# A hybrid diffusion block on one core: the first FFN's last two blocks go down in one PSUM group, a third raw-weight buffer in the late heads, and the last norm divides before its transposes

## The chip, the cores and the metric

The kernel runs on one core of a Trainium2 chip. The metric is the device time of one execution, in microseconds (us), and the time shown is the median over several runs. A profile of one further execution gives the start and the length of each instruction on each engine. PE is TensorE (its weight loads are PEld), DVE is VectorE, ACT is ScalarE, POOL is GpSimd, and SP is SyncE, which here only issues transfers.

## The reference, cut to what matters

Two layers are computed over 512 latent tokens (x) and 256 context tokens (c) of width 1024. In the second layer the context is only read, and it gets no output.

```python
for l in range(DEPTH):                       # DEPTH = 2
    hx = _modulate(_rmsnorm(x, norm1_g[l]), sh1, sc1)
    hc = _modulate(_rmsnorm(cx, norm1_g[l]), csh1, csc1)
    ... = _split_heads(hx @ w_in[l], ...)     # w_in: 1024 x 2560
    x = x + g1 * _merge(na_x, diff_x, fux, ..., w_out[l])
    x = x + g2 * _conv_ffn(_modulate(_rmsnorm(x, norm2_g[l]), sh2, sc2), w_up[l], ..., w_down[l])
    if l < DEPTH - 1:                         # the same for the context tokens
        ...
def _conv_ffn(h, w_up, conv_w, conv_b, w_down):
    u = h @ w_up                              # w_up: 1024 x 5632
    u = up[:, :-2] * conv_w[0] + up[:, 1:-1] * conv_w[1] + up[:, 2:] * conv_w[2] + conv_b
    gate, val = jnp.split(u, 2, axis=-1)
    return (jax.nn.silu(gate) * val) @ w_down # w_down: 2816 x 1024
```

The six modulation vectors of a layer (sh1, sc1, g1, sh2, sc2, g2) come from `silu(c) @ w_mod[l] + b_mod[l]`, with w_mod 1024 x 6144.

## The kernel before, in words

Every large product is made of three matmuls: each operand is split into a rounded high part and the remainder as a low part (`split`: a cast on ACT, a subtraction on DVE or POOL), and high by high, high by low and low by high are summed in PSUM (`PASS`). Raw weights arrive by 1 MB transfers on SP's queue into tiles named `w`, which come from a pool `wp` of two buffers through a small class `Turn` that takes its pools in turn.

The instructions are not issued in program order. A planner orders each engine's instructions ahead of time by their place in the program and by times that it reckons; `tc.high_priority(tc.cur_priority - mark + ...)` moves a piece forward to the place noted in `mark`. On the chip each engine and each queue then takes its instructions strictly in the planned order.

**The modulation.** `w_mod` is multiplied in chunks of 512 columns (`mod_chunk`), two `w` tiles for each (`hf` 0 and 1) and eight small matmuls for each tile. `filler` does one chunk and finishes the chunk before it (`mod_finish`, line L184); it is called here and there to put this work between other work.

**The late heads.** The last four of the eight neighbourhood heads run while the modulation chunks for later use are multiplied (12 `w` tiles in layer 0, 8 in layer 1), followed by the four tiles of `w_out` (`out_weights`, L963). When they begin, the projection's buffers are closed and the freed memory goes to new pools (L1147 to L1159). Behind the heads, SP also loads six residual tiles in layer 0 (L1205), and then the output projection runs (L1233).

**The norms.** `norm_T` normalises token tiles and transposes them into 128-column pieces `k` = 0 to 7. The sum of squares is made on ACT (`stats`), and `spread` turns it into the reciprocal root `r`, spreads `r` along the tokens by a diagonal matrix and a matmul with ones (`bank`, L384) and copies it out (`rb`). For every `k`, `lift` transposes on PE, and `step` multiplies by `rb` and then by the modulation on DVE, casts the high part on ACT (L419) and makes the low part on POOL (L420), or on DVE for `k` = 3 and 7. In the second norm of layer 1 the tiles 0 to 2 go first (384 tokens) and tile 3 follows (128 tokens).

**The FFN.** It has 22 blocks `f` of 128 hidden columns, taken in pairs `j` = 0 to 10. `up_mm` makes `u` (x) and, in layer 0, `uc` (c); `conv` makes the gated product `gt` on ACT and DVE. `down` loads a pair's `w_down`, splits it into `wd`, and for each token tile (in layer 0 the two context tiles first, then the four x tiles) and each half of the columns sums six matmuls into one PSUM bank `dps`. The bank is multiplied by the gate into `dm` on DVE (L1362) and added to the residual `res` on POOL for the first half and on DVE for the second (L1363). Three banks are there for `dps` in layer 0, shared with the fillers. `down` of pair `j - 1` stands behind the up products of pair `j`; `down(9)` and `down(10)` are thus the last two, and behind them the first norm and projection of layer 1 begin (`bank`, L529: `hc` for context and `hx` for x).

Of the kernel before, what the change touches and what calls it, by code (L numbers as in the profile page):

```python
# [11 lines left out]
F32 = mybir.dt.float32  # L12
# [8 lines left out]
D = 1024  # L21
# [3 lines left out]
DEPTH = 2  # L25
# [24 lines left out]
def hybrid_kernel(ctx: ExitStack, tc: tile.TileContext, A, out, dbg=None, stop=None):  # L50
# [293 lines left out]
    def norm_T(l, which, xnp, hx, hc, pn, bank, wrap, cuts=((0, 4),), htile=None):  # L344
        hT = {0: [(hx[z] if isinstance(hx, list) else hx).tile([128, KT, 576 if wrap else 512], F32R, name=f"hx{z}")
                  for z in range(2)]}
        if hc:
            hT[1] = [hc.tile([128, KT, 256], F32R, name=f"hc{z}") for z in range(2)]
        tiles, ss, rb, tps = {}, {}, {}, {}

# [19 lines left out]
        def spread(v, i0, i1):  # L370
            n = i1 - i0
            x0 = xnp.tile([128, n], F32, tag=f"nx{n}", name="nx")
            ve.tensor_scalar(x0, ss[v][:, 0, i0:i1], 1.0 / D, EPS, op0=ALU.mult, op1=ALU.add)
            x = xnp.tile([128, n], F32, tag=f"ny{n}", name="ny")
            ve.scalar_tensor_tensor(x, ss[v][:, 1, i0:i1], 1.0 / D, x0, op0=ALU.mult, op1=ALU.add)
            r = rsqrt(x, "v" if which == 2 else None)
            if v not in rb:
                rb[v] = xnp.tile([128, 256 if v else 512], F32, tag=f"rb{v}", name="rb")
            dg = xnp.tile([128, 3, 128], F32, tag="dg", name="dg")[:, 0:n]
            ve.tensor_tensor(dg, idf.unsqueeze(1).to_broadcast([128, n, 128]),  # L380
                             r.unsqueeze(2).to_broadcast([128, n, 128]), op=ALU.mult)
            bc = bank(v)
            for i in range(n):
                pe.matmul(place(bc, v, i0 + i), lhsT=ones, rhs=dg[:, i], start=True, stop=True)  # L384
            cut_ = (lambda t: t[:, 0:256]) if v else CUT[i0, i1]
            sc.copy(cut_(rb[v]), cut_(bc))

        def lift(k, v, part=0):
            if (k, v, part) not in tps:
                tp = tps[k, v, part] = pn.tile([128, 256 if v else 512], F32, tag="n", name="ntp")  # L390
                for i in range(2) if v else range(*cuts[part]):
                    pe.transpose(place(tp, v, i), tiles[v][i][:, k * 128:(k + 1) * 128], idf)

        def step(k, v, part=0):
            lift(k, v, part)
            cut_ = (lambda t: t[:, 0:256]) if v else CUT[cuts[part]]
            tp, r = cut_(tps[k, v, part]), cut_(rb[v])
            n = 256 if v else 128 * (cuts[part][1] - cuts[part][0])
# [8 lines left out]
            w3 = [hT[0][z][:, k, 512:576] for z in range(2)] if wrap and v == 0 else []  # L407
            if k % 4 == 3:
                ve.scalar_tensor_tensor(h, tp, A_, r, op0=ALU.mult, op1=ALU.mult)
# [19 lines left out]
        def begin_x(xs):  # L429
            stats(0, xs)  # L430
            spread(0, 0, 3)
            lift(0, 0)
            spread(0, 3, 4)
# [24 lines left out]
    for l in range(DEPTH):  # L458
# [516 lines left out]
        with ExitStack() as es:  # L975
# [166 lines left out]
            for n, (h, i) in enumerate(steps):  # L1142
# [3 lines left out]
                if (he, ie) == (4, 0):  # L1146
# [9 lines left out]
                    open_rows(es, f"rp{l}", side="right")  # L1156
                    tqs.append(pool(es, f"tr{l}", 1, side="right"))
                    pt.pools += [pt.pools[0], pool(es, f"ptr{l}", 1, space=PSUM, side=SR)]
                    po.pools += [po.pools[0], pool(es, f"por{l}", 1, space=PSUM, side=SR)]  # L1159
# [31 lines left out]
            if first:  # L1191
                load_gate(g1, l, 2)

        es_att.close()
# [54 lines left out]
        with ExitStack() as es:  # L1249
# [91 lines left out]

            def down(j, gt):
                nonlocal mark
                w = wtile([128, 2, D])
                nc.sync.dma_start(w, A["w_down"][l, j * 256:(j + 1) * 256].rearrange("(k p) f -> p k f", p=128))
                wd = []
                for ff in range(2):
                    t = wdl.tile([128, 2, D], F32R, tag="wd", name="wd")
                    split(t[:, 0], t[:, 1], w[:, ff])
                    wd.append(t)  # L1350
                for t, key in order:
                    if t == 0:
                        mark = tc.cur_priority
                    for ch in range(2):
                        cs_ = slice(ch * 512, (ch + 1) * 512)
                        ps = pd.tile([128, 512], F32, tag="d", name="dps")
                        for ff in range(2):
                            for z, (a, b) in enumerate(PASS):
                                pe.matmul(ps, lhsT=gt[:, ff, a, t * 128:(t + 1) * 128], rhs=wd[ff][:, b, cs_],  # L1359
                                          start=ff == 0 and z == 0, stop=ff == 1 and z == 2)  # L1360
                        m = dmp.tile([128, 512], F32, tag="dm", name="dm")
                        ve.tensor_tensor(m, ps, g[:, 0 if key[0] == "x" else 1, cs_], op=ALU.mult)  # L1362
                        (gp if ch == 0 else ve).tensor_tensor(res[key][:, cs_], res[key][:, cs_], m, op=ALU.add)  # L1363
# [45 lines left out]
            for j in range(nj + 1):  # L1409
                if j < nj:  # L1410
# [3 lines left out]
                    for f in (2 * j, 2 * j + 1):  # L1414
# [8 lines left out]
                        elif f == 9:  # L1423
                            bias_scratch(l + 1, m)
                        elif f and f % 2 == 0:
                            filler((pd, "d"))
                            if f == 2:
                                filler((pd, "d"))
                if j > 0:
                    down(j - 1, gts[j - 1])  # L1430
        if dbg:
# [98 lines left out]
```

## Time and the profile before

| | |
|---|---|
| median of 3 runs | 1895.62 us (1895.04 to 1897.27) |
| the profiled execution's own time | 1893.96 us |
| its span, first to last instruction | 1892.2 us |
| PE busy | 1790.1 us (95% of the span) |
| DVE, ACT, POOL busy | 1284.0, 731.6 and 619.9 us |
| mean granted PE clock | 0.977 of full speed |

The profiled execution is 1.66 us (0.09%) below the median. Some 1.8 us of its time lie outside its span. Times of instructions are counted from the span's start: layer 0's attention ends at about 444, its output projection at 514, its FFN at 1117; layer 1's output projection runs from 1453 to 1498 and its FFN to the end.

### The profile page before, as it was taken

How to read it: one execution, taken by the hardware profiler on the slowest of the kernel's cores; microseconds unless marked ns; L12 is line 12 of the kernel's file. 1: busy time of each engine (PE TensorE's matmuls, PEld its weight loads, DVE VectorE, ACT ScalarE, POOL GpSimd, SP SyncE). 2: the span in 40 equal slices, each digit the busy share in tenths (PEclk: the TensorE clock that was granted, in tenths of full speed). 3: DMA queues.
4: the chain of work that ended last, by engine and by line, in shares of the span. 5: the costliest groups of instructions: out<-in, count | busy, mean ns of one | idle time of the engine just before them, and what ended most of it. 6: DMA issues, size and time to landing. Idle time of an engine off the chain costs nothing.

```text
span 1892.2 us, 27838 instructions
## 1 busy us (share of the span) xinstructions
PE 1790.1 (95%) x10817; PEld 1495.8 (79%) x10817; DVE 1284.0 (68%) x2561; ACT 731.6 (39%) x1335; POOL 619.9 (33%) x798
## 2 busy tenths in 40 slices
PE   6988999988999999999999989899999999999997
PEld 4787889856877888888888868788986778888885
DVE  4575865576465776677777695586658568777775
ACT  3325755454244222222232243475545243333331
POOL 2454646432141211211111154464733232122122
PEclk7998999999999999999999999999999999999999
DMA  9350021167015323423333012202234333232311
GB/s 282 118 177 24 31 55 32 34 211 209 28 45 187 126 95 103 161 73 106 112 112 112 23 51 95 89 24 61 55 110 137 100 112 112 89 112 90 94 41 45
DMA packets 146715, 183.04 MB, mean 97 GB/s; under 512 B 38200, under 2 KB 108672, under 8 KB 145560
## 3 DMA queue, kind: packets, MB, share of 16 engines
q1 hardware_dynamic: 107056, 157.83, 26.0%
q0 software_dynamic: 5888, 20.26, 3.5%
q10 hardware_dynamic: 33640, 3.19, 1.4%
q8 instruction: 85, 1.39, 0.3%
q14 instruction: 46, 0.38, 0.1%
HBM read 179.07 MB, written 8.07 MB: 99 GB/s over the span
## 4 chain that ended last, share of the span: by engine, by line
PE 79%; DVE 7%; DMA 6%; ACT 2%; issue 2%; POOL 2%; SPq 0%; ACTq 0%; DVEq 0%; POOLq 0%
PE u L1295 25%; PE dps L1359 14%; PE nacc L645 11%; PE uc L1295 7%; PE oacc L1233 5%; DMA w<-w_in 2%; PE bank L529 2%; PE m L143 2%; PE o L712 2%; PE s L1078 2%; DMA w<-w_out 2%; PE do L712 1%; PE tpp L1109 1%; PE dtpp L874 1%; PE ds L839 1%
## 5 line engine op out<-in xcount | busy, mean ns | idle before, releaser
L1295 PE MATMUL u<-hx,uwh 128*128 128x512 f32 (+2 forms) x2160 | 513.8, 391 | 7.1 <-ACT hx L419 2.7
L1295 PEld LDWEIGHTS u<-hx,uwh 128*128 128x128 f32 x2160 | 401.1, 189 | 98.0 <-ACT hx L419 3.6
L1363 POOL TENSOR_TENSOR res<-res,dm 128x512 f32<-128x512 f32 x110 | 157.3, 1431 | 586.1 <-DVE dm L1362 580.4
L1359 PE MATMUL dps<-wd,gt 128*128 128x512 f32 x1320 | 321.7, 393 | 6.8 <-DVE wd L75 3.0
L1359 PEld LDWEIGHTS dps<-wd,gt 128*128 128x128 f32 x1320 | 247.4, 189 | 62.8 <-DVE dm L1362 4.5
L645 PE MATMUL nacc<-wh,hx 128*128 128x256 f32 x1536 | 213.4, 291 | 3.8 <-ACT wh L71 3.1
L1324 DVE SCALAR_TENSOR_TENSOR ob<-u,cvc,ob 128x504 f32<-128x504 f32 x352 | 152.8, 476 | 89.7 <-ACT ob L1321 88.7
L645 PEld LDWEIGHTS nacc<-wh,hx 128*128 128x128 f32 x1536 | 196.7, 195 | 9.0 <-ACT wh L71 3.5
L1362 DVE TENSOR_TENSOR dm<-dps,g 128x512 f32<-128x512 f32 x220 | 147.7, 683 | 57.7 <-PE dps L1359 52.5
L1321 ACT ACTIVATE ob<-u,cvc 128x512 f32<-128x512 f32 x88 | 68.2, 777 | 195.8 <-PE u L1295 195.8
L1295 PEld LDWEIGHTS uc<-hc,uwh 128*128 128x128 f32 x1056 | 130.9, 190 | 7.4 <-issue 1.7
L1295 PE MATMUL uc<-hc,uwh 128*128 128x256 f32 x1056 | 134.3, 284 | 1.1 <-POOL hc L420 0.5
L75 POOL TENSOR_TENSOR wh<-w,wh 128x512 fp32r<-128x512 f32 x70 | 94.4, 1362 | 56.6 <-ACT wh L71 56.5
L71 ACT CAST uwh<-w 128x1024 fp32r<-128x1024 f32 x88 | 90.9, 1042 | 38.2 <-DMA w<-w_up 25.5
L1233 PE MATMUL oacc<-owh,yh 128*128 128x512 f32 x320 | 98.8, 397 | 5.9 <-ACT yh L71 3.2
L75 DVE TENSOR_TENSOR uwh<-w,uwh 128x1024 fp32r<-128x1024 f32 x74 | 97.0, 1317 | 8.8 <-ACT uwh L71 7.3
L1324 DVE SCALAR_TENSOR_TENSOR ob<-uc,cvc,ob 128x248 f32<-128x248 f32 (+1 forms) x176 | 53.0, 341 | 52.1 <-ACT ob L1320 51.5
L1363 DVE TENSOR_TENSOR res<-res,dm 128x512 f32<-128x512 f32 x110 | 87.2, 793 | 1.6
L645 PE MATMUL nacc<-wh,hc 128*128 128x256 f32 x624 | 88.1, 293 | 0.0
L71 ACT CAST gt<-g 128x768 fp32r<-128x768 f32 (+1 forms) x44 | 32.0, 727 | 136.5 <-DVE g L1339 136.5
L71 ACT CAST wd<-w 128x1024 fp32r<-128x1024 f32 x44 | 44.8, 1048 | 97.9 <-PE dps L1359 69.5
L645 PEld LDWEIGHTS nacc<-wh,hc 128*128 128x128 f32 x624 | 80.1, 196 | 2.7 <-issue 1.9
(527 smaller groups left out, 2872.7 us busy)
## 6 DMA issues: line engine op xcount, KB each, us to landing
w<-w_up SPq DMA_DIRECT2D x44, 1024.0 KB, 5.2
w<-w_mod SPq DMA_DIRECT2D x40, 1024.0 KB, 6.6
w<-w_down SPq DMA_DIRECT2D x22, 1024.0 KB, 5.0
w<-w_in SPq DMA_DIRECT2D x18, 1024.0 KB, 5.2
wm<-w_mod SPq DMA_DIRECT2D x8, 1024.0 KB, 9.9
w<-k_dftx POOLq DMA_DIRECT2D x8, 1024.0 KB, 5.2
w<-w_out SPq DMA_DIRECT2D x8, 1024.0 KB, 12.7
bS<-bT POOLq DMA_DIRECT2D x16, 360.0 KB, 9.1
```

What stands on the lines that cost most here:

```text
L71: r = sc.copy(dh, src)
L75: (gp if lo == "p" else ve).tensor_tensor(dl, src, dh.bitcast(F32), op=ALU.subtract)
L143: pe.matmul(m[32 * k:32 * k + 32, :], lhsT=cm[:, hf * 4 + k, :], rhs=w[:, k, :], start=hf == 0, stop=hf == 1)
L645: m = pe.matmul(acc[:, j], lhsT=col(hT[a], k, t + j), rhs=whs[k // 2][:, k % 2, b], start=k == 0 and z == 0, stop=k == KT - 1 and z == 2)
L712: m = pe.matmul(o[64 * half:64 * half + 64, 128 * b:128 * b + 128], lhsT=v, rhs=r, start=n == 0, stop=n == len(jobs) - 1)
L1233: pe.matmul(accs[t], lhsT=ys[k][a][:, t * 128:(t + 1) * 128], rhs=ow0[k // 2][:, k % 2, b], start=n == 0 and z == 0, stop=n == KT - 1 and ...
L1295: m = pe.matmul(u[2][:, 256 * v:256 * v + 256] if c else cut(u[v]), lhsT=whs[v][:, b, k], rhs=h2[c][a][:, k] if c else cut(h2[c][a][:, k]) ...
L1321: sc.activation(ob[:, 0:512], xu, AF.Identity, bias=b_, scale=w1)
L1324: ve.scalar_tensor_tensor(ob[:, d0:d0 + n], src[:, s0:s0 + n], w_, ob[:, d0:d0 + n], op0=ALU.mult, op1=ALU.add)
L1359: pe.matmul(ps, lhsT=gt[:, ff, a, t * 128:(t + 1) * 128], rhs=wd[ff][:, b, cs_], start=ff == 0 and z == 0, stop=ff == 1 and z == 2)
L1362: ve.tensor_tensor(m, ps, g[:, 0 if key[0] == "x" else 1, cs_], op=ALU.mult)
L1363: (gp if ch == 0 else ve).tensor_tensor(res[key][:, cs_], res[key][:, cs_], m, op=ALU.add)
```

## The change

Three edits are made at once.

The first is in layer 0's FFN. `down` is divided into `down_w` (load and split) and `down` (matmuls). The weights of pair 9 are prepared in their usual place, the weights of pair 10 go into the memory of the x tokens' low parts (`h2[0][1]`), and one `down` sums twelve matmuls to a bank for both pairs together. The fillers that stood behind blocks 18 and 20 move behind block 21, after `down_w(9)`.

The second is in both layers' late heads: a pool `wr` with one more raw buffer is appended to `wps`, so that tiles come in turn from `wp` and `wr`, and it is taken off again behind the heads.

The third is in the second norm of layer 1 (`early`). Each token tile is multiplied by its `r` on ACT, in two passes of 512 columns, into `xt`; the transposes read `xt`; `step` then has one DVE operation in front of the cast. The diagonal matrix, its matmuls and `rb` are not made there.

```diff
+        early = l == DEPTH - 1 and which == 2
...
             r = rsqrt(x, "v" if which == 2 else None)
+            if early:
+                for i in range(i0, i1):
+                    xt[v, i] = xnp.tile([128, D], F32, name=f"xt{v}{i}")
+                for c in range(0, D, 512):
+                    for i in range(i0, i1):
+                        sc.activation(xt[v, i][:, c:c + 512], tiles[v][i][:, c:c + 512], AF.Copy,
+                                      scale=r[:, i - i0:i - i0 + 1])
+                return
...
+            if early:
+                ve.tensor_scalar(h, tp, A_, B_, op0=ALU.mult, op1=ALU.add)
+                sc.copy(hi, h)
+                (ve if k % 4 == 3 else gp).tensor_tensor(lo, h, hi.bitcast(F32), op=ALU.subtract)
...
             spread(0, 0, 3)
-            lift(0, 0)
+            if not early:
+                lift(0, 0)
             spread(0, 3, 4)
...
+                    wps.pools.append(pool(es, f"wr{l}", 1, side="right"))
...
+            wps.pools[:] = [wp]
...
-            def down(j, gt):
+            def down_w(j, ts=None):
...
-                    t = wdl.tile([128, 2, D], F32R, tag="wd", name="wd")
+                    t = ts[:, ff] if ts else wdl.tile([128, 2, D], F32R, tag="wd", name="wd")
...
+            def down(wd):
...
-                        for ff in range(2):
+                        for n, (w, gt) in enumerate(wd):
...
-                        elif f and f % 2 == 0:
+                        elif f and f % 2 == 0 and f < 18:
...
-                if j > 0:
-                    down(j - 1, gts[j - 1])
+                if last or j < nj - 1:
+                    if j > 0:
+                        down(down_w(j - 1))
+                elif j < nj:
+                    wd = down_w(j - 1)
+                    while mods or late:
+                        filler((pd, "d"))
+                else:
+                    down(wd + down_w(j - 1, h2[0][1].rearrange("p (f z k) c -> p f z (k c)", f=2, z=2)))
```

## Rows read from the trace of the kernel before

**Rows 1.** Stretches: busy us (and instructions) of each engine, PE clock, DMA share, GB/s.
```profile
470.00:480.00 10.00, 9.87 (x36) 7.91 (x37) 6.31 (x10) 1.91 (x4) 0.00 (x0) 0.83 0.66 210
...
1076.20:1096.40 20.20, 16.96 (x73) 13.01 (x72) 19.24 (x32) 5.89 (x10) 7.11 (x5) 1.00 0.14 47
...
1117.20:1133.60 16.40, 12.48 (x90) 11.52 (x90) 14.94 (x39) 7.82 (x23) 6.42 (x8) 0.90 0.01 1
...
1498.10:1519.40 21.30, 17.12 (x81) 13.64 (x82) 17.92 (x39) 8.26 (x17) 8.84 (x9) 0.84 0.63 212
```

**Rows 2.** PE in order of time, layer 0's FFN end: start, length, count, [idle before].
```profile
1006.27 1.92 PE L143 MATMUL m<-w,cm 128*32 128x512 f32 x16
...
1103.10 14.07 PE L1359 MATMUL dps<-wd,gt 128*128 128x512 f32 x60 [0.21 <-DVE wd L75]
...
1133.57 2.09 PE L529 MATMUL bank<-wh,hx 128*128 128x512 f32 x8
```

**Rows 3.** Groups by line, 1076 to 1124: count, busy us, mean ns, idle before.
```profile
L1363 POOL TENSOR_TENSOR res<-res,dm 128x512 f32<-128x512 f32 x12 | 16.5, 1380 | 45.2 <-DVE dm L1362 39.6 <-DVE nx L373 2.4 <-DVE rt__10966 L311 2.0
L1362 DVE TENSOR_TENSOR dm<-dps,g 128x512 f32<-128x512 f32 x24 | 15.8, 680 | 1.3 <-PE dps L1359 1.1
L1363 DVE TENSOR_TENSOR res<-res,dm 128x512 f32<-128x512 f32 x12 | 11.0, 925 | 0.1
...
L75 DVE TENSOR_TENSOR wd<-w,wd 128x1024 fp32r<-128x1024 f32 x2 | 4.3, 2141 | 0.0
L71 ACT CAST wd<-w 128x1024 fp32r<-128x1024 f32 x2 | 2.0, 1046 | 8.0 <-PE dps L1359 8.0
```

**Rows 4.** ACT and DVE in order of time: the convolution of blocks 20 and 21.
```profile
1058.86 0.56 ACT L1320 ACTIVATE ob<-uc,cvc 128x256 f32<-128x256 f32 x1 [4.99 <-PE uc L1295]
1064.50 0.96 DVE L75 TENSOR_TENSOR gt<-g,gt 128x768 fp32r<-128x768 f32 x1 [0.90 <-ACT gt L71]
1076.23 0.56 ACT L1320 ACTIVATE ob<-uc,cvc 128x256 f32<-128x256 f32 x1 [4.96 <-PE uc L1295]
1086.09 1.45 DVE L75 TENSOR_TENSOR gt<-g,gt 128x768 fp32r<-128x768 f32 x1
```

**Rows 5.** Transfers by line: count, KB each, median us from issue to landing.
```profile
w<-w_down SPq DMA_DIRECT2D x22, 1024.0 KB, 5.0
w<-w_mod SPq DMA_DIRECT2D x12, 1024.0 KB, 9.4
```

**Rows 6.** PE in order of time: layer 0's late heads and output projection.
```profile
408.92 1.67 PE L143 MATMUL m<-w,cm 128*32 128x512 f32 x8 [4.05 <-DMA w<-w_mod]
...
470.13 0.78 PE L1233 MATMUL oacc<-owh,yh 128*128 128x512 f32 x2 [2.67 <-DVE om L1238]
```

**Rows 7.** SP's queue in order of time: issues of raw weight tiles.
```profile
399.44 0.37 SPq L140 DMA_DIRECT2D w<-w_mod  x1
...
445.69 0.38 SPq L967 DMA_DIRECT2D w<-w_out  x1
...
1402.55 1.23 SPq L140 DMA_DIRECT2D w<-w_mod  x2
```

**Rows 8.** PE in order of time: layer 1's second modulation chunk.
```profile
1407.81 1.07 PE L143 MATMUL m<-w,cm 128*32 128x512 f32 x8
1411.13 1.06 PE L143 MATMUL m<-w,cm 128*32 128x512 f32 x8
```

**Rows 9.** PE in order of time: the second norm of layer 1.
```profile
1501.50 2.29 PE L1295 MATMUL u<-hx,uwh 128*128 128x384 f32 x6 [2.28 <-ACT hx L419]
...
1518.07 3.75 PE L1295 MATMUL u<-hx,uwh 128*128 128x512 f32 x20 [0.39 <-ACT hx L419]
```

**Rows 10.** Groups by line and form, 1498 to 1535: count, busy us, mean ns.
```profile
L420 POOL TENSOR_TENSOR hx<-h,hx 128x384 fp32r<-128x384 f32 x6 | 7.7, 1297 | 10.3 <-ACT hx L419 8.3 <-issue 2.0
...
L417 DVE TENSOR_TENSOR h<-ntp,rb 128x384 f32<-128x384 f32 x6 | 3.2, 552 | 1.7 <-PE ntp L392 1.6
...
L367 ACT ACTIVATE h<-res 128x512 f32<-128x512 f32 x1 | 0.6, 630 | 0.2 <-DVE res L1239 0.2
```

More of the change, by code (lines that the diff above doesn't have):

```diff
@@ L348, in norm_T @@
             hT[1] = [hc.tile([128, KT, 256], F32R, name=f"hc{z}") for z in range(2)]
-        tiles, ss, rb, tps = {}, {}, {}, {}
+        tiles, ss, rb, tps, xt = {}, {}, {}, {}, {}
+        early = l == DEPTH - 1 and which == 2
         def place(t, v, i):
@@ L391, in lift @@
                 for i in range(2) if v else range(*cuts[part]):
-                    pe.transpose(place(tp, v, i), tiles[v][i][:, k * 128:(k + 1) * 128], idf)
+                    pe.transpose(place(tp, v, i), xt.get((v, i), tiles[v][i])[:, k * 128:(k + 1) * 128], idf)
         def step(k, v, part=0):
@@ L396, in step @@
             cut_ = (lambda t: t[:, 0:256]) if v else CUT[cuts[part]]
-            tp, r = cut_(tps[k, v, part]), cut_(rb[v])
+            tp = cut_(tps[k, v, part])
+            r = None if early else cut_(rb[v])
             n = 256 if v else 128 * (cuts[part][1] - cuts[part][0])
@@ L407, in step @@
             w3 = [hT[0][z][:, k, 512:576] for z in range(2)] if wrap and v == 0 else []
-            if k % 4 == 3:
+            if early:
+                ve.tensor_scalar(h, tp, A_, B_, op0=ALU.mult, op1=ALU.add)
+                sc.copy(hi, h)
+                (ve if k % 4 == 3 else gp).tensor_tensor(lo, h, hi.bitcast(F32), op=ALU.subtract)
+            elif k % 4 == 3:
                 ve.scalar_tensor_tensor(h, tp, A_, r, op0=ALU.mult, op1=ALU.mult)
@@ L1340, in conv @@
                 split(gt[:, ff, 0], gt[:, ff, 1], g32)
-            def down(j, gt):
-                nonlocal mark
+            def down_w(j, ts=None):
                 w = wtile([128, 2, D])
@@ L1347, in down @@
                 for ff in range(2):
-                    t = wdl.tile([128, 2, D], F32R, tag="wd", name="wd")
+                    t = ts[:, ff] if ts else wdl.tile([128, 2, D], F32R, tag="wd", name="wd")
                     split(t[:, 0], t[:, 1], w[:, ff])
-                    wd.append(t)
+                    wd.append((t, gts[j][:, ff]))
+                return wd
+            def down(wd):
+                nonlocal mark
                 for t, key in order:
@@ L1356, in down @@
                         ps = pd.tile([128, 512], F32, tag="d", name="dps")
-                        for ff in range(2):
+                        for n, (w, gt) in enumerate(wd):
                             for z, (a, b) in enumerate(PASS):
-                                pe.matmul(ps, lhsT=gt[:, ff, a, t * 128:(t + 1) * 128], rhs=wd[ff][:, b, cs_],
-                                          start=ff == 0 and z == 0, stop=ff == 1 and z == 2)
+                                pe.matmul(ps, lhsT=gt[:, a, t * 128:(t + 1) * 128], rhs=w[:, b, cs_],
+                                          start=n == 0 and z == 0, stop=n == len(wd) - 1 and z == 2)
                         m = dmp.tile([128, 512], F32, tag="dm", name="dm")
```

## The prediction

> **What bounds the kernel now.** I read the table of stretches first: it shows in which stages PE, the busiest engine, is short of work. It is full through the FFN's blocks, and short in three places that the change touches. From 1076 to 1096 and from 1117 to 1134 it has 17.0 of 20.2 and 12.5 of 16.4 us, and DVE is all but full [rows 1]. In the norm before the last FFN it has 17.1 of 21.3 us at a clock of 0.84 [rows 1]. In layer 0's late heads it waits 4.05 us for a `w_mod` tile, and 2.67 us for a gate product before the second half of the output projection [rows 6]. The rest of the chain of waits is PE itself, so a saving elsewhere is worth something only where it ends one of these waits. The time order of PE and the groups by line say which operations end them.
>
> A difference of 0.2%, 3.8 us, is about what a measurement of this kernel tells from no change.
>
> **The joint down of pairs 9 and 10.** Removed: twelve `dm` at 0.680 and six residual additions at 0.925 on DVE, 13.7 us, and six at 1.38 on POOL, 8.3 us [rows 3]. The matmuls stay: 144 of them, at 14.07 / 60 = 0.235 us [rows 2], are 33.8 us. Today PE works on pair 9 while block 21 is convolved, then waits for banks that DVE empties late and for the second `wd`; the downs end at 1103.10 + 14.07 = 1117.2, and the first x matmul of layer 1 stands at 1133.57 [rows 2].
>
> After: the last chunk's sixteen matmuls (1.92 us, now at 1006) [rows 2] move behind block 21. PE's sum is the same; the up products end 1.9 us earlier, at 1076.2 - 1.9 = 1074.3 (the convolution's pass at 1076.23 starts as they end) [rows 4], and PE does the chunk until 1076.2. It can do pair 9's part of three banks, 18 matmuls or 4.2 us, until 1080.4. Then it needs two things.
>
> First, pair 10's `gt`. Block 20 took from 1058.86 to 1064.50 + 0.96, 6.6 us, behind its last up product; block 21 took from 1076.23 to 1086.09 + 1.45, 11.3 us, because DVE emptied banks in between [rows 4]. So `gt` is there between 1080.9 and 1085.6.
>
> Second, pair 10's `wd`. Its raw tile waits for the buffer of the moved chunk's first half, released about 1.0 us into the chunk, at 1075.3; a `w_down` tile takes 5.0 us [rows 5]; cast and low part take 1.05 and, beside a working POOL, 2.14 us [rows 3]. The first half stands at 1080.3 + 3.2 = 1083.5, and its high part alone at 1081.4. I take a wait of 3 us, from 1080.4 to 1083.4; the ends are 1 us, and 10 us if the tile takes the 9.4 us of a `w_mod` tile [rows 5] and the splits stand behind other work. The remaining 126 matmuls take 29.6 us: 1113.0.
>
> The context tiles come first in a down. Their four banks are done some 22 us before the end, and DVE, 13.7 us lighter, can then do the context's norm during the x tiles' matmuls; about 2 us of its transposes move there too: 1115. Behind the end remain the context's products (most of the 12.5 us of PE's stretch from 1117 to 1134, some of it at a lower clock [rows 1]; I take 8) and the chain of the last x tile from gate product to first high part. That chain is 16.4 us now, with the context's norm on DVE between its links; in the norm of layer 1, from the last output bank at 1498.1, the first product came at 1501.5 and the part with the last tile some 9 us behind the bank. So x starts at 1115 + 9 = 1124 against 1133.6: **-9.5 us**. As the planner sets the order, I count **-8**. The most is PE's idle time in these stretches and what the slow clock took, -12; the least is 0, with the 10 us wait.
>
> **The third raw buffer, layer 0.** The tile PE waited for was issued at 399.44 [rows 7], when the chunk before had released its buffer, and landed at 408.9 [rows 6]. In turn between `wp` and `wr`, first halves all go to `wp` and find a buffer two chunks early: that one would be issued some 12 us sooner, and the wait of 4.05 us goes. The last `w_out` tile is issued at 445.69, behind the six residual tiles [rows 7]; its split holds DVE, and the gate product behind it holds PE 2.67 us [rows 6]. With the buffers of the last chunk and the first `w_out` tile free earlier it can go ahead of the residuals, and that wait goes too. Behind it PE ran at 0.83 from 470 to 480 [rows 1], 1.7 us of work lost at the lower of its two levels. The Trainium skill ("TensorE: Matmul & The Clock Gate", on the clock gate) says that slow is the default state and that activity lifts it; by that rule the 1.7 us go with the wait, and the trace agrees in having the low clock just behind it. Sum -8.4 at most, -6.7 without the clock.
>
> Against it: `wr` lies in memory that the projection uses until about 375, so the second half of the first chunk, loaded long before today, comes after that, and SP's queue behind it waits as well: the next first half, then residuals and weights in their order. PE has head work to put there. The cost lies between nothing and one landing, 5 us. I take **-5** for layer 0.
>
> **Layer 1's late heads** show no wait for a tile. Half of the first chunk is late here as well, and `w_out` is some 8 us earlier. I take **0**, between -2 and +3.
>
> **The last norm.** Removed: the diagonal matrix, its matmuls, `rb`, and one DVE operation of 0.55 us in six of eight steps [rows 10]. Added: eight ACT passes. The nearest row is the sum of squares over the same 512 columns, 0.63 us [rows 10]. Three passes give the first transposes, so the first high part could come at 1500.8; if ACT runs all six first, about 1.9 us later, at 1502.5. Today the first product is at 1501.50 [rows 9]: -0.7 to +1.0. The gain is in the flow: today the matmuls of tile 3's broadcast stand ahead of the transposes for `k` = 1, so the eight steps end at about 1519. Without them the steps are paced by POOL's low parts, six at 1.3 = 7.8 us [rows 10], or by PE, 48 matmuls of 384 columns and transposes, about 10 us. From 1502 this gives 1512, and 1514.5 with the two splits that DVE does in the same stretch: -4.5. I count **-3.5**, between +1 and -7.
>
> The Trainium skill ("ScalarE: Activation LUTs", rules for kernel authors) puts a multiplication on VectorE, not on ScalarE. By that rule the eight passes sit on the wrong engine and become the norm's pace. ACT is busy for 8.3 of the 21.3 us [rows 1], which speaks against it, and the first six passes in one stream speak for it.
>
> **Sum.** -8 - 5 + 0 - 3.5 = -16.5. The profiled execution takes 1893.96, so 1877.5; it stands 1.7 below the median, so the median becomes **1879**.
>
> **The rivals.**
> *The joint down starves.* DVE's relief is paid for with the 13 us in which pair 9 covered block 21's convolution; with the wait at 10 instead of 3 us, and the clock low behind it, the first edit gives 0: 1879 + 8 = 1887. For it: the tile's late issue. Against it: 5.0 us is the median of 22 such loads. Chance 0.15.
> *The third buffer shows nothing*, because the late second half gives back what the early first halves gain: 1884. Chance 0.12.
> *ScalarE paces the norm*, edit three gives 0: 1882.5. Chance 0.10.
> *Every second half goes through one buffer.* In turn, all second halves use `wr`. A chunk then can't be shorter than one landing and one half's matmuls. Two tiles issued together at 1402.55 [rows 7] were used at 1407.81 and 1411.13 [rows 8], so the first of a pair lands in 5.2 us, and a chunk of 6.5 us is hidden. If instead each took 11 us, between the 9.4 of rows 5 and 12.7 for `w_out` on the page, six chunks from 375 would end at 375 + 6 x 12.4 = 449 against 433 now, and four in layer 1, from 1400, at 1450 against 1438: +28, less 11.5 from the other edits: 1895.6 + 16 = 1912. It decides from about 9.8 us per load. Chance 0.08.
> *The planner gives it back:* another order of the same work, with new waits as long as the old: 1894. Chance 0.10.
> The forecast itself: 0.45.
>
> **How the numbers follow.** The forecast, its three small variants and all of the starving case but its tail are faster by over 3.8 us: 0.45 + 0.15 + 0.12 + 0.10 = 0.82, less 0.02: 0.80. Within 0.2%: 0.10 + 0.02 = 0.12. Slower: 0.08. The forecast's bounds are 1895.6 - 27 = 1868 (all parts at their best) and 1887 (first edit at nothing). With the case of no change above it the range is 1868 to 1894: below it is nearly nothing, above it the slow case and half of the unchanged one.
>
> **What would show it.** Right: no wait of PE for a `w_mod` tile in the heads, the last `w_out` tile issued before the residuals, twelve `dm` fewer, the first x product of layer 1 some 15 us earlier and the part behind it unchanged, the eight norm steps ended within 14 us of the last output bank. Wrong: PE waiting over 5 us between the last up product and the joint down, m matmuls waiting for second halves, or ACT full between 1497 and 1505.

## The result and the profile after

The changed kernel takes 1875.15 us (median of 4 runs, 1874.01 to 1877.31), the kernel before in the same session 1896.44 us: a ratio of 0.9885, with a 95% interval from 0.9870 to 0.9899, or 21 us less. Forecast were 1879 us, with 0.80 for a gain. The profiled execution takes 1875.44 us, 18.5 less than the profiled one of before.

The stretches that answer to [rows 1], in the same order (after the second half of the output projection begins; end of the first FFN; the products behind it; last norm):

```profile
466.80:476.80 10.00, 10.00 (x43) 8.13 (x44) 4.66 (x7) 2.40 (x3) 1.62 (x1) 1.00 0.33 105
1068.40:1088.60 20.20, 18.43 (x89) 13.26 (x90) 15.40 (x31) 11.97 (x23) 5.97 (x5) 1.00 0.49 170
1108.60:1119.10 10.50, 9.54 (x80) 9.10 (x79) 9.53 (x24) 5.88 (x20) 4.78 (x6) 1.00 0.01 2
1482.10:1503.40 21.30, 19.34 (x107) 16.78 (x107) 15.27 (x31) 12.50 (x25) 8.54 (x10) 0.92 0.66 223
```

PE is the second column. It is fuller in all four. DVE (the fourth) is emptier in all but the third, where it stays at 0.91 of the stretch, and ACT (the fifth) is up by 4.2 us in the last one.

PE in order of time at the end of the first FFN, for [rows 2]:

```profile
1068.31 1.92 PE L143 MATMUL m<-w,cm 128*32 128x512 f32 x16
...
1071.52 4.37 PE L1379 MATMUL dps<-wd,gt 128*128 128x512 f32 x18
1075.72 0.86 PE L1379 MATMUL dps<-hx,gt 128*128 128x512 f32 x3
1076.83 3.76 PE L1379 MATMUL dps<-hx,gt 128*128 128x512 f32 x15 [0.24 <-DVE hx L75]
1081.84 1.65 PE L1379 MATMUL dps<-wd,gt 128*128 128x512 f32 x6 [1.25 <-DVE dm L1382]
...
1107.07 1.54 PE L1379 MATMUL dps<-hx,gt 128*128 128x512 f32 x6
1119.08 2.12 PE L544 MATMUL bank<-wh,hx 128*128 128x512 f32 x8 [0.45 <-ACT hx L433]
```

The moved chunk, then three banks of pair 9, then pair 10 from the tile that was `hx`: the order that the prediction drew. PE waits 0.24 us for pair 10's weights and 1.25 us for a bank, not 3. The gate product and the second halves of the weights on ACT and DVE, in order of time:

```profile
1074.46 2.00 ACT L71 CAST hx<-w 128x1024 fp32r<-128x1024 f32 x2 [2.87 <-DMA w<-w_down]
1076.37 0.83 ACT L71 CAST gt<-g 128x768 fp32r<-128x768 f32 x1
...
1075.55 2.36 DVE L75 TENSOR_TENSOR hx<-w,hx 128x1024 fp32r<-128x1024 f32 x2 [1.96 <-ACT hx L71]
1077.82 0.95 DVE L75 TENSOR_TENSOR gt<-g,gt 128x768 fp32r<-128x768 f32 x1
```

The low part of `gt` stands at 1078.8, 10.4 us behind the last up product; in [rows 4] it took 11.3 us. The gate product itself (`g`) is whole at 1073.6, but on ACT its cast stands behind the casts of pair 10's weights, which wait 2.87 us for their raw tile; so the chain is hardly shorter than before. The two splits take 1.2 us each, not the 2.14 of [rows 3]: POOL is idle beside them, and in the kernel before it was splitting `wh` beside them (from 1098.07 to 1105.44). By line, from 1068 to 1125, twelve `dm` are left of 24:

```profile
L1382 DVE TENSOR_TENSOR dm<-dps,g 128x512 f32<-128x512 f32 x12 | 8.1, 687 | 3.3 <-PE dps L1379 3.2
L1383 POOL TENSOR_TENSOR res<-res,dm 128x512 f32<-128x512 f32 x6 | 7.8, 1293 | 50.2 <-DVE dm L1382 40.7 <-DVE rt__11095 L311 4.9 <-DVE h L431 4.6
L1383 DVE TENSOR_TENSOR res<-res,dm 128x512 f32<-128x512 f32 x6 | 5.2, 873 | 0.1
```

Layer 0's late heads on PE, and the queue of SP behind them, for [rows 6, 7]:

```profile
402.63 1.06 PE L143 MATMUL m<-w,cm 128*32 128x512 f32 x8
406.19 1.06 PE L143 MATMUL m<-w,cm 128*32 128x512 f32 x8
...
428.92 0.37 SPq L982 DMA_DIRECT2D w<-w_out  x1
429.35 3.18 SPq L333 DMA_DIRECT2D res<-x  x5
...
443.36 0.38 SPq L982 DMA_DIRECT2D w<-w_out  x1
```

No modulation product waits for its tile any more. But the last `w_out` tile still stands behind the residual tiles: it is issued at 443.36, when POOL's split of an earlier `w_out` tile ends. And the low clock has moved to the start of the output projection, where the first eight products take 3.62 us, against 2.12 at full clock in the kernel before. POOL's split, these products, and the stretch from 440 to 450:

```profile
438.66 4.67 POOL L75 TENSOR_TENSOR owh<-w,owh 128x1024 fp32r<-128x1024 f32 x2 [9.77 <-ACT owh L71]
```

```profile
442.36 3.62 PE L1250 MATMUL oacc<-owh,yh 128*128 128x512 f32 x8 [1.42 <-ACT yh L71]
```

```profile
440.00:450.00 10.00, 8.30 (x35) 6.54 (x35) 8.44 (x10) 8.34 (x11) 3.33 (x2) 0.83 1.04 196
```

Where the 18.6 us between the two profiled spans lie, each stretch taken between the same instructions on PE:

| Stretch | before | after | difference |
|---|---|---|---|
| start to the first score of layer 0's heads | 278.73 | 281.17 | +2.4 |
| from there to the first FFN | 240.25 | 232.83 | -7.4 |
| first FFN to layer 1's first product on `x` | 614.59 | 605.08 | -9.5 |
| from there to layer 1's output projection | 319.48 | 316.71 | -2.8 |
| output projection of layer 1 | 45.00 | 46.35 | +1.4 |
| its last bank to the first down of the last FFN | 62.47 | 58.19 | -4.3 |
| from there to the last down | 321.66 | 323.22 | +1.6 |

No edit lies in the first stretch; in the fourteen profiles it takes 277.2 to 282.2 us.

### The profile page after: what moved, and what is told of

Its sections match the earlier page's. It is cut to its first block, busy times and chain, and to the rows that moved or that the text cites. A ratio compares the mean times of both kernels' runs of the same rounds, so it can differ in the third digit from the quotient of the medians.

```text
span 1873.6 us, 27783 instructions
## 1 busy us (share of the span) xinstructions
PE 1784.2 (95%) x10809; PEld 1492.4 (80%) x10809; DVE 1262.0 (67%) x2529; ACT 734.8 (39%) x1341; POOL 609.6 (33%) x792
## 4 chain that ended last, share of the span: by engine, by line
PE 80%; DVE 6%; DMA 5%; issue 3%; ACT 3%; POOL 2%; SPq 0%; ACTq 0%; POOLq 0%; DVEq 0%
PE u L1312 25%; PE dps L1379 15%; PE nacc L660 12%; PE uc L1312 7%; PE oacc L1250 4%; DMA w<-w_in 4%; PE o L727 2%; PE m L143 2%; PE bank L544 2%; PE s L1093 2%; PE tpp L1124 2%; PE do L727 1%; PE dtpp L889 1%; PE ds L854 1%; PE u L759 1%
## 5 line engine op out<-in xcount | busy, mean ns | idle before, releaser
L1383 POOL TENSOR_TENSOR res<-res,dm 128x512 f32<-128x512 f32 x104 | 151.2, 1454 | 587.2 <-DVE dm L1382 577.7
L1379 PE MATMUL dps<-wd,gt 128*128 128x512 f32 x1248 | 306.2, 393 | 3.1 <-DVE wd L75 1.4
L1379 PEld LDWEIGHTS dps<-wd,gt 128*128 128x128 f32 x1248 | 234.3, 189 | 54.4 <-DVE dm L1382 1.8
L1382 DVE TENSOR_TENSOR dm<-dps,g 128x512 f32<-128x512 f32 x208 | 140.1, 685 | 63.4 <-PE dps L1379 59.5
L1383 DVE TENSOR_TENSOR res<-res,dm 128x512 f32<-128x512 f32 x104 | 81.4, 783 | 1.7
```

The lines of the kernel that those rows point to most:

```text
L1379: pe.matmul(ps, lhsT=gt[:, a, t * 128:(t + 1) * 128], rhs=w[:, b, cs_], start=n == 0 and z == 0, stop=n == len(wd) - 1 and z == 2)
```

## The experiments

Each kernel's ratio is to the kernel before, timed in the same rounds; the stretches are those of the table.

**One edit at a time.** The first four kernels hold one edit each, the others of the change undone.

The joint down alone:

```diff
-        early = l == DEPTH - 1 and which == 2
+        early = False
...
-                    wps.pools.append(pool(es, f"wr{l}", 1, side="right"))
```

> The kernel before with the joint down of pairs 9 and 10 alone. If the stretches of the two traces can be added up, this is worth what lies between the last up product of the first FFN and the first product of layer 1: -9.9 us (1886). The prediction's term was -8. Rival: the joint down needs the buffers of the other edit (an earlier raw tile, another phase of the buffers); then it gives less than -5. In the trace: PE waits 1 to 2 us in all between the last up product and the joint down, and the first layer-1 product on the x tokens comes some 10 us earlier than before.

Measured: 0.9947 (0.9934 to 0.9960), -10 us. From the first FFN to layer 1's first product it takes 606.96 us, 7.6 less than before. The other 1.9 of the changed kernel's 9.5 is the clock: here it is 0.91 in the first 40 us of the FFN, behind which every product is 2.0 us later, and 1.00 there in both other kernels. The edit needs nothing of the others.

The third buffer alone, in layer 0 (with 1 for 0: in layer 1), with `early` false and each pair going down by itself:

```diff
-                    wps.pools.append(pool(es, f"wr{l}", 1, side="right"))
+                    if l == 0:
+                        wps.pools.append(pool(es, f"wr{l}", 1, side="right"))
```

> The kernel before with the third raw buffer in layer 0's late heads alone. Read from the two traces: -6.9 us by the start of the FFN, 4.05 of it the wait for the w_mod tile, the rest the gate product and the clock behind it (1889). The prediction's term was -5. Rival: only the 4.05 us wait goes and the rest of the 6.9 us belongs to the run, not to the edit: -4.

> The kernel before with the third raw buffer in layer 1's late heads alone. Read from the two traces: -2.4 us, because the owh split of the last heads falls 23 us earlier and no longer stretches DVE's softmax at the end (1893.2). The prediction's term was 0, between -2 and +3. Rival: the 2.4 us came with layer 0's edit (the order carried over) and this one is within 1 us of the kernel before.

Measured: 0.9945 (0.9933 to 0.9957), -10 us, for layer 0, and 0.9988 (0.9975 to 1.0000), -2 us, for layer 1. Layer 0 gives more than the -6.9 us of the expectation. The reason is in the kernels without the buffer: from the first score to the output projection they took 165.8 us (the profile of before), 166.0, 170.1 and 170.9, with a wait of 4.05 to 4.58 us for the `w_mod` tile in each; those with it, in both of this change's layers or in layer 0, 161.2 to 164.7. From the first score to the FFN the four take 240.3 to 246.9 us, and the nine with it (its turns not exchanged) 231.7 to 236.2. Where 170 us were needed, the clock was low around the wait (0.83 and 0.66 in two stretches of 10 us in the kernel with the early norm alone). The profiled execution of before was one of the good ones.

For layer 1, DVE in order of time in the kernel before shows what went (`sb` is the softmax's last multiplication; the 31 of its 64 beside which POOL does nothing take 0.47 to 0.49 us each):

```profile
1440.87 2.55 DVE L1089 TENSOR_SCALAR sb<-sb,rr 128x512 f32<-128x512 f32 x1
...
1443.53 2.38 DVE L1089 TENSOR_SCALAR sb<-sb,rr 128x512 f32<-128x512 f32 x1
```

and POOL beside it, before, and then in the kernel with layer 1's buffer alone:

```profile
1440.76 4.86 POOL L75 TENSOR_TENSOR owh<-w,owh 128x1024 fp32r<-128x1024 f32 x2 [7.72 <-ACT owh L71]
```

```profile
1443.31 4.91 POOL L75 TENSOR_TENSOR owh<-w,owh 128x1024 fp32r<-128x1024 f32 x2 [9.04 <-ACT owh L71]
```

POOL's split of `w_out` and DVE's multiplication ran into each other 12.3 us ahead of the output projection (1453.05), on PE's last products of the heads: a wait of 1.86 us. With the buffer the split is 18.2 us ahead of it (1461.55) and the last wait for `sb` is 0.42 us. (That is 6 us earlier against the work around it, not the 23 us of the expectation, which compared the two traces' clocks.) The Trainium skill ("SBUF — State Buffer", on the two separate sides) says that GpSimd and a VectorE operation in a two-port mode, or with two SBUF inputs, shut each other out of a shared port pair for a whole instruction. The 2.4 to 2.6 us against 0.49, beside splits of 2.4 us, agree with it; that this multiplication runs in such a mode no row shows.

The size is less sure than this reason. The interval reaches 1.0000, and the kernel with the buffer in layer 0 alone, which has none here, takes 315.92 us from layer 1's first product on `x` to its output projection, 3.6 less than before. There the split begins 9.6 us ahead of the projection, two multiplications take 0.84 and 1.45 us and PE waits 1.08 and 0.66 us for them, and the clock in these last 10 us is 1.00, against 0.83 before. So an execution can be rid of this wait and of its low clock in part without the buffer. With the turns exchanged (below) the buffer is there, but the split comes 11.9 us ahead of the projection, a multiplication takes 3.07 us and the wait is 1.89 us again: what counts is when the split falls.

The early norm alone:

```diff
-                    wps.pools.append(pool(es, f"wr{l}", 1, side="right"))
...
-                if last or j < nj - 1:
+                if True:
...
-                        elif f and f % 2 == 0 and f < 18:
+                        elif f and f % 2 == 0:
```

> The kernel before with the early division in the last norm alone. Read from the two traces: -2.9 us by the start of the conv of the second block (1892.7); the first product comes 4.2 us after the last output bank instead of 3.4, and the clock in the 22 us behind the bank is higher (0.92 instead of 0.84). The prediction's term was -3.5. Rival: the higher clock came with the other edits, and this one alone gives -1 us or less.

Measured: 0.9981 (0.9969 to 0.9993), -3.6 us; from the last bank to the first down 57.54 us, 4.9 less than before. The four differences are -10.1, -10.4, -2.3 and -3.6, in all -26, each known to 2.4 us; the whole change gave -21 (19 to 25). They add up within that.

**The joint down: fewer evictions, or the place behind block 21?** The same order as the changed kernel, with banks of its own for each pair:

```diff
-                    down(wd + down_w(j - 1, h2[0][1].rearrange(...)))
+                    wd2 = down_w(j - 1, h2[0][1].rearrange(...))
+                    down(wd)
+                    down(wd2)
```

> The changed kernel with the order of the joint down but with banks apart: both pairs go down behind block 21, first all twelve banks of pair 9, then all twelve of pair 10, so DVE and POOL do the twelve evictions more again; PE's work is the same. If the gain of this edit (-9.7 us) is DVE's relief, this gives most of it back: the first product of layer 1 comes 7 to 10 us later than in the changed kernel, and DVE has nearly no idle time between block 21 and the end of the downs (total 1883). If it is the place behind block 21 (gate chain covered by the last chunk and by pair 9), at most 3 us are lost (1878).

Measured: 0.9904 (0.9885 to 0.9923), 1880 us. Layer 1's first product on `x` comes 612.62 us behind the FFN's first, 7.5 later than in the changed kernel and 2.0 earlier than before. From 1085 to 1105:

```profile
1085.00:1105.00 20.00, 17.13 (x71) 12.96 (x71) 19.62 (x24) 4.92 (x12) 14.81 (x11) 1.00 0.25 82
```

DVE is full again and PE waits three times for a bank in it. The downs end 2.2 us later than in the changed kernel, and `x` begins 15.8 us behind them instead of 10.5, because DVE comes to the context's norm later. So in the traces 7.5 us of the 9.5 are the twelve spared evictions, and 2 us the order. The timed ratios differ by 3.6 us, in the same direction, but by less than their intervals can tell.

**The joint down in the last FFN too**, where DVE has less to do:

```diff
-                if last or j < nj - 1:
+                if j < nj - 1:
```

> The changed kernel with the joint down of the last two pairs in the last FFN as well, where DVE has no norm and no context tiles to do. If the joint down pays by the evictions that it spares a full DVE, it has little to spare here, and it takes away cover: today PE has pair 9's 48 matmuls (11.3 us) under the convolution of block 21, a chain of about 10 us, and waits 0.5 us for a bank; joined it has 24 (four banks, 5.6 us), so it waits 4 to 5 us and the kernel is 2 to 4 us longer than the changed one (1878). If the joint down pays by itself (fewer banks, no end of a down to wait for), this one gains as well: 1 to 2 us (1874).

Measured: 0.9851 (0.9836 to 0.9866), 1870.4 us: a gain where I expected a loss. PE at the end of the changed kernel, then PE and DVE in this one:

```profile
1837.51 11.09 PE L1379 MATMUL dps<-wd,gt 128*128 128x512 f32 x48
1849.06 1.20 PE L1379 MATMUL dps<-wd,gt 128*128 128x512 f32 x4 [0.46 <-ACT wd L71]
1851.67 0.60 PE L1379 MATMUL dps<-wd,gt 128*128 128x512 f32 x1 [1.41 <-DVE wd L75]
```

```profile
1837.32 1.55 PE L1379 MATMUL dps<-wd,gt 128*128 128x512 f32 x6
...
1843.56 1.55 PE L1379 MATMUL dps<-wd,gt 128*128 128x512 f32 x6
1844.94 3.64 PE L1379 MATMUL dps<-hx,gt 128*128 128x512 f32 x15
...
1837.59 1.23 DVE L75 TENSOR_TENSOR hx<-w,hx 128x1024 fp32r<-128x1024 f32 x1 [1.57 <-PE u L1312]
1841.94 0.69 DVE L75 TENSOR_TENSOR gt<-g,gt 128x512 fp32r<-128x512 f32 x1 [0.69 <-ACT gt L71]
```

I had counted the cover that is lost and kept the chain behind it at its old length. But the chain was long because evictions stood between its links: here `gt` is whole 5.1 us after the last up product (7.6 in the changed kernel), before the four banks run out, and the second `wd`, which was late by 0.46 and 1.41 us, is ready because it has a tile of its own. From the last up product to the last down it takes 22.52 us, against 24.27 with the old order at full clock. That is 1.7 us. The timed ratios lie 6.4 us apart, and 3.2 from the second sample of the changed order (below); where more than the 1.7 us comes from is not shown.

**Which buffer's turn.** The new buffer takes the first halves instead of the second ones:

```diff
-                    wps.pools.append(pool(es, f"wr{l}", 1, side="right"))
+                    wps.pools.insert(0, pool(es, f"wr{l}", 1, side="right"))
```

> The changed kernel with the two buffers' turns exchanged: the new raw buffer takes the first halves of the late heads' chunks, the old pool the second ones. If the gain lies in the first halves that find a free buffer early (the prediction's reason), the first tile of the first chunk now waits for the memory that the projection leaves at about 375, and PE waits for a w_mod tile again: 2 to 5 us more in layer 0's late heads (1878 to 1880). If any third buffer does it, the start of the first FFN stays within 1 us (1875).

Measured: 0.9895 (0.9875 to 0.9915), 1878.8 us. PE in layer 0's late heads:

```profile
393.90 1.92 PE L143 MATMUL m<-w,cm 128*32 128x512 f32 x16
404.98 1.94 PE L143 MATMUL m<-w,cm 128*32 128x512 f32 x8 [4.19 <-DMA w<-w_mod]
```

The wait of [rows 6] is back, and from the first score to the output projection it takes 166.25 us again, against 161.19 in the changed kernel. The output projection up to the FFN keeps its gain (71.87 us; 74.47 before). The timed loss, 1.9 us by the ratios, is too small to stand out of the intervals. So the two parts of the gain are apart: the first halves that are there early end the wait in the heads; any third buffer gives the part behind them.

**The last norm: which engine, and when.** The eight multiplications on DVE; the second 512 columns on POOL; and the second 512 columns behind the high part of `k` = 1 on ACT, first by their place in the program alone, then (the last diff, on top of that one, with `cast` for the high part's instruction) tied to that high part:

```diff
-                        sc.activation(xt[v, i][:, c:c + 512], tiles[v][i][:, c:c + 512], AF.Copy,
-                                      scale=r[:, i - i0:i - i0 + 1])
+                        ve.tensor_scalar(xt[v, i][:, c:c + 512], tiles[v][i][:, c:c + 512],
+                                         r[:, i - i0:i - i0 + 1], None, op0=ALU.mult)
```

```diff
+                        if c:
+                            gp.tensor_scalar(xt[v, i][:, c:c + 512], tiles[v][i][:, c:c + 512],
+                                             r[:, i - i0:i - i0 + 1], None, op0=ALU.mult)
+                            continue
```

```diff
-                for c in range(0, D, 512):
-                    for i in range(i0, i1):
+                halve(i0, 0)
...
+                if k == 1:
+                    halve(cuts[part][0], 512)
```

```diff
-                    halve(cuts[part][0], 512)
+                    halve(cuts[part][0], 512, cast)
```

> The changed kernel with the eight multiplications of the last norm on DVE instead of ACT (the two engines exchanged for them, nothing else). In the changed kernel the first high part waits on ACT behind six passes of 0.63 us and a square of 0.8 us: its h is there at 1484.5 and the cast starts at 1485.75. If ACT's queue is what delays the first product (the rival 'ScalarE paces the norm', and the Trainium skill's placing of multiplications on VectorE), it comes about 1 us earlier than 4.2 us behind the last output bank, and the time to the first down of the last FFN (58.2 us from the last output bank) is some 1 us shorter. If DVE is the scarcer engine there (it makes every h, some low parts and tile 3's root), the six passes at about 0.5 us each, 2.9 us, stand in front of the first h and of each later one: 1 to 3 us longer, and the gain of the last norm (-4.3 us against before) shrinks to half. Total 1875 to 1878.

> The changed kernel with the second 512 columns multiplied on POOL, which has nothing to do until the first low part. Like the delayed passes if POOL's passes (1.0 to 1.4 us each by its other 512-column operations, three of them 3 to 4 us) end before the first low part is due: first product 1.2 us earlier, first down up to 1.2 us earlier, 1874. If POOL paces the steps, its first low parts move 1 to 2 us back and the first down of the last FFN is up to 2 us later: 1877.

> The changed kernel with the second 512 columns of the tiles multiplied on ACT only after the high part of k = 1, instead of in one stream of six passes. If the stream of six is what delays the first product, that product comes 1.2 us earlier (3.0 us behind the last output bank instead of 4.2), and the first down of the last FFN comes up to 1.2 us earlier: 1874. If the flow behind it sets the pace (DVE's h, PE's own matmuls), the start moves and the first down does not: 1875, within 0.5 us.

> The changed kernel with the second 512 columns of three tiles multiplied behind the high part of k = 1 on ACT, tied to it by an order on the engine (the kernel with the late halves alone ran in the very order of the changed kernel, because the schedule put the passes into ACT's free time). If the stream of six passes delays the first product, it comes 1.2 us earlier than 4.2 us behind the last output bank and the end comes up to 1.2 us earlier. If the flow behind it sets the pace, the first product moves and the last 384-column product (18 to 19 us behind the bank) does not: within 0.5 us of the changed kernel, save for where the low clock falls, which moved the same order of instructions by 3 us in this stretch.

| Kernel | ratio (interval) | first product, us behind the bank | last 384-column product ends | first down |
|---|---|---|---|---|
| changed | 0.9885 (0.9870 to 0.9899) | 4.16 | 17.72 | 58.19 |
| on DVE | 0.9882 (0.9864 to 0.9899) | 4.37 | 19.41 | 61.50 |
| half on POOL | 0.9877 (0.9860 to 0.9894) | 3.04 | 20.30 | 60.65 |
| late by place | 0.9868 (0.9850 to 0.9886) | 4.17 | 17.76 | 61.45 |
| late by order | 0.9871 (0.9848 to 0.9894) | 3.02 | 17.15 | 59.48 |

The kernel that is late by place has every engine's instructions in the very order of the changed one, so it is a second sample of it, and yet its first down is 3.3 us later. The clock did half of that. Its windows, then those of the changed kernel (12 us behind the bank, and 12 us from 30 us behind it):

```profile
1483.80:1495.80 12.00, 9.50 (x54) 7.62 (x54) 10.66 (x23) 9.37 (x18) 4.52 (x5) 1.00 0.65 220
1513.80:1525.80 12.00, 10.10 (x42) 7.84 (x42) 6.72 (x16) 8.30 (x10) 6.54 (x3) 0.88 0.02 4
```

```profile
1482.10:1494.10 12.00, 10.25 (x52) 8.80 (x52) 10.63 (x23) 9.40 (x18) 4.49 (x5) 0.86 0.66 220
1512.10:1524.10 12.00, 10.11 (x46) 7.89 (x46) 8.12 (x18) 9.00 (x11) 8.15 (x4) 1.00 0.00 1
```

In the changed kernel the low clock fell on the stretch where PE waits for the norm anyway and cost nothing: two more profiles with this very order (banks apart, and the joint down in the last FFN), at full clock throughout, come to the first down at 58.69. In the kernel late by place it fell on a stretch of full PE and cost 1.6 us. The other 1.6 us come from a late tile. ACT starts to cast the `w_down` tile 9.3 us behind its issue instead of 7.3, a high part stands behind that cast, and PE waits for it:

```profile
1506.02 2.00 ACT L71 CAST wd<-w 128x1024 fp32r<-128x1024 f32 x2 [5.73 <-DMA w<-w_down]
```

```profile
1508.27 4.04 PE L1320 MATMUL u<-hx,uwh 128*128 128x128 f32 x21 [1.00 <-ACT hx L426]
```

So the column of the first down can't rank the variants by less than some 3 us, and the timed ratios don't tell them apart either. What they do show: late by order brings the first product 1.14 us forward, as half on POOL does, and its last 384-column product ends at 17.15 us, 0.6 earlier than in the samples of the changed order (17.72 to 17.76 in four). So the stream of six passes does hold up the first product, half of that is left at the end of these products, and the rest of the pace is set by the flow behind it. (The 18 to 19 us of the expectation are the ends of rows in which products of 512 columns follow.) Half on POOL shows one thing that paces it: beside POOL's low parts, now later by their engine's passes, one step of tile 3's root holds DVE for 3.36 us, and every `h` behind it.

```profile
1488.48 3.36 DVE L310 TENSOR_TENSOR rt__15566<-ry 128x1 f32<-128x1 f32 x1
```

On DVE a pass takes 0.41 us (six in 2.47), on ACT 0.63; the Trainium skill's rule for multiplications ("ScalarE: Activation LUTs", rules for kernel authors) is right about the single operation, but the kernel's time doesn't change: all six passes stand ahead of DVE's first `h`, which starts 3.0 us behind the bank instead of 1.8.

**All that helped**, the joint down in both FFNs with the second halves late by order (on top of the kernel that is late by place):

```diff
-                if last or j < nj - 1:
+                if j < nj - 1:
...
-                    halve(cuts[part][0], 512)
+                    halve(cuts[part][0], 512, cast)
```

> The joint down in both FFNs, and the second halves of the last norm's multiplications behind the high part of k = 1. The joint down in the last FFN gained where a loss was expected: with no evictions on DVE the convolution of block 21 and its gate product took 5.3 us instead of 8.6, so four banks covered it, and the two waits for the last wd (0.46 and 1.41 us) were gone. If it repeats, this kernel takes 1869 to 1871, as with the joint down alone; with the earlier first product of the norm up to 1.2 us less.

Measured: 0.9849 (0.9826 to 0.9872), 1870.2 us. It is level with the joint down in the last FFN alone (0.9851); the norm's order adds nothing that can be measured. Both lie below the changed kernel's 0.9885 and, by less than their intervals, below its second sample (0.9868). In the trace the gain at the end is 1.7 us at equal clock. (The 5.3 and 8.6 us of the expectation are 5.1 and 7.6, measured from the end of the last up product.)

## Why the prediction was right

**The sum.** Forecast -16.5 us, -18.5 between the profiled executions, -21 between the medians. The direction, the order of the terms and their reasons held, except where named. That the total came so close is in part luck: the four stretches of the change gave 24.0 us where 16.5 were counted, and 5.4 us in the three others, none of them an edit's, took most of the difference back.

**The joint down: right, and closer to the working than to the number taken.** Worked out -9.5, counted -8; measured -9.5 in the table and -10 alone. Its links came as drawn, with small ones that cancelled. The raw tile was issued 1.1 us into the moved chunk, at 1069.43, and landed 5.0 us later, as in [rows 5]. The wait for the second `wd` was 0.24 us, not 3, because the split took 1.2 us instead of 2.14, three of pair 10's products need the high part alone, and pair 9's part ran to 7.3 us behind the last up product instead of 6.1 (two transposes of the chunk's rows stand in front of it). A bank was late by 1.25 us, which was not counted, and `x` began 10.5 us behind the downs' end (1108.6), not 9. The starving rival counted on a late tile; there was none. The sign for it (PE idle over 5 us) didn't come.

**The third buffer in layer 0: right in kind, the size too small.** Counted -5; -7.4 in the table, -10 alone. The turn of the buffers was the reason given, and exchanging the turns brings the wait of 4 us back. The 5 us set against it, for a late second half, cost nothing that PE shows. The clock was counted behind the second wait only; kernels before also lose it behind the first. The 1.7 us that were to go with the second wait did not go in the profiled execution: the clock is 1.00 there now, but low at the start of the projection, 1.5 us on its first eight products, as in eight of the ten profiles with this buffer. In the other two it is 1.00 throughout, and the projection up to the FFN takes 70.19 us instead of 71.64. One link was wrong: the last `w_out` tile did not go ahead of the residuals. It is issued 1 us behind the start of the output projection in both kernels (445.69 and 443.36, against 444.51 and 442.36), in both when POOL's split of an earlier `w_out` tile ends (445.02 and 443.33), so a buffer that is free earlier did not move it. The residuals themselves are issued 11 us earlier, 429.35 instead of 440.77, and the tile's second halves are split on DVE from 455.91, not from 467.00 as in

```profile
467.00 2.36 DVE L75 TENSOR_TENSOR owh<-w,owh 128x1024 fp32r<-128x1024 f32 x2 [12.81 <-ACT owh L71]
```

of the kernel before, which is just ahead of the gate product that PE waited for. That the residuals' bytes held up the tile behind them fits these times; no run moved the residuals alone.

**Layer 1's heads: a term missed.** Counted 0; -2.3 alone, with an interval that reaches 0, and -2.8 in the table. I looked for a wait on a tile and found none. The wait that went was one for DVE's softmax, which POOL's split of a weight stretched until the earlier tile moved it; how much of the gain is this wait and how much the clock behind it stays open.

**The last norm: the size right, the pace behind the start wrong.** Counted -3.5; -4.3 in the table and -3.6 alone. The six profiles with the six passes in one stream on ACT come to the first down 57.5 to 61.5 us behind the bank, 59.2 in the mean, the four without the early norm at 62.5. The first product was put at -0.7 to +1.0 against before and came at +0.7, behind all six passes and the square of the last tile. The sign, eight steps ended within 14 us, missed: the last low part of 384 columns stood at 15.5 us, and the last of the products at 17.7. The first term was the right sort of bound (ACT), the pace was not POOL's low parts alone, but DVE as well: `h` at 0.67, two splits and the root of tile 3. The ScalarE rival held for 1.1 us of the start, of which 0.6 were left at the last 384-column product, and for nothing that the timed ratios show.

**The rest.** That planner and clock take nothing back was assumed. The clock took 1.4 us in layer 1's output projection and 1.6 us at the end, on the same instructions with the same waits.

## What to carry to other kernels

Where the matrix engine waits at the end of a stage for banks to be emptied, let two blocks share the banks. Where evictions stood between the links of the chain that the waiting was meant to cover, as in the last FFN, sparing them shortens that chain, so count it anew instead of keeping its old length. Look for a late tile in the order of the buffers' turns before looking at bandwidth. And price a saving of a few us by a whole stage in more than one profile: a low clock on a full instead of an idle stretch moved the same instructions by 1.6 us here, and together with one late tile by 3.3.

## What the runs showed of the hardware

The granted clock falls low in different places in executions of the same order of instructions. At the end of the kernel it is 0.92 and 0.91 in the last two 10 us of downs of the changed kernel, and 1.00 in both for the second sample of the same order, with waits of equal length: 25.88 against 24.26 us from the last up product to the last down.

```profile
1843.60:1853.60 10.00, 8.13 (x32) 6.01 (x31) 9.72 (x11) 2.00 (x2) 3.74 (x3) 0.92 0.00 0
1853.60:1863.60 10.00, 9.95 (x40) 7.77 (x39) 6.75 (x10) 0.00 (x0) 4.61 (x3) 0.91 0.27 68
```

```profile
1846.90:1856.90 10.00, 8.13 (x35) 6.11 (x34) 9.96 (x13) 2.62 (x3) 3.88 (x3) 1.00 0.01 2
1856.90:1866.90 10.00, 9.95 (x44) 7.88 (x42) 8.11 (x12) 0.00 (x0) 4.61 (x3) 1.00 0.26 68
```

POOL's work beside DVE's can hold up a short operation by more than its own length: the softmax's multiplication took 0.47 to 0.49 us without it and up to 3.07 us beside a split on POOL (in the kernel with the turns exchanged), and a step of the root on 128x1 numbers 3.36 us beside three low parts.
